# Block sums of the hidden state stored as high and low parts; value products in three passes

## The chip, the cores and the metric

One core of a Trainium2 chip runs the whole program in one launch. The metric is the time on the device in microseconds, the median of the runs. The core has five engines that matter here: TensorE (PE) multiplies matrices into PSUM; VectorE (DVE), ScalarE (ACT) and GpSimd (POOL) work elementwise, POOL without access to PSUM; SyncE (SP) issues the DMAs, in the order in which they stand in its queue. Each engine runs its own instructions in order and waits on semaphores for the others.

## The reference

A block of two layers works on 1024 tokens of width 1024, with 256 tokens of context ahead of them in the first layer. Everything is 32-bit floating point. What the change touches lies in the first layer:

```python
def mlstm_features(h, w_in, conv_w, conv_b, w_q, w_k, w_v):
    xm, z, og = jnp.split(h @ w_in, 3, axis=-1)
    xc = jax.nn.silu(short_conv(xm, conv_w, conv_b))
    q = headwise(xc, w_q)
    k = headwise(xc, w_k) * (MLSTM_HEAD_DIM ** -0.5)
    v = headwise(xm, w_v)
    return q, k, v, xc, z, og
...
    pre = (qkv @ w_g + b_g).astype(jnp.float32)
...
    y = jax.nn.sigmoid(og) * hn + skip * xc
    return (y * jax.nn.silu(z)) @ w_out
```

`h` is the normalised and modulated input, `headwise` a product with a block-diagonal matrix of 4 x 4 blocks. Four heads of width 512 then attend over the tokens, weighted with decays that come from the gates `pre`, forwards and backwards. The second layer (a pooling mixer) is not touched.

## The kernel before

**Products.** A matmul takes 32-bit operands that were rounded to a shorter type. To keep precision, each operand is held as a high part (the rounded value) and a low part (what the rounding left), and a product is three matmuls into one PSUM bank: high x high, high x low, low x high (`mm3`, L136). Each matmul has its own weight load, also where it repeats the one before. A weight tile is loaded from DRAM (tag `wr`), rounded on ACT (`wh`, L139), and DVE subtracts to get `wl` (L141).

**Stages.** The start-up (0 to 83 us) loads and normalises the input and modulates it on ACT and DVE (`modulate`, L306). The features follow (to some 355 us): 16 tiles `n` of 128 columns of `xm`, each a product over eight blocks of `h`, then a convolution. Behind tile `n`, `token_part(n)` makes the values and the gates' share of its tokens; it is a generator, and its pieces are put between the products of tile `n + 1` (one piece per six matmuls). A piece of 128 tokens is one matmul of 288 columns (high part against both parts of the weights) and one of 144; DVE adds the two halves out of PSUM (L400) into a tile of tag `T5`, and a store puts the 16 tiles into `v_d`. POOL adds `h` up from its parts in tiles 2 to 9 (L503) and SP stores it in `h_d`.

The plain stage (to some 411 us) makes the first two tiles of `z` and of `og` in the ordinary way. Between its products run the last token part, the steps of the gates (`gates`, at the counts `GATE_STEPS` of finished k-blocks: a chain of small DVE instructions, L442 to L453, then 20 transposes on PE, L460, which ACT copies out, L461, then scans on DVE) and `sums` at the counts `SUM_STEPS`: it loads `h_d` back into `T5` tiles (L516) and makes four block sums, each with high and low part (L520 to L527), in tiles `T_`.

The other 14 tiles of `z` and of `og` are made two at a time by `strassen` (to some 692 us): seven block products instead of eight, from two weight tiles `r1` (tag `wr`, L538) and `r2` (tag `T5`, L539) and sums of their blocks, which POOL makes (L543 to L546); each product's weights are rounded by ACT (L553) and DVE (L554).

Attention (692 to 1252 us) goes over four heads with eight query tiles each. In a head's first tile its `xc` is rounded (`cast_x`: ACT L651, and for heads 1 to 3 POOL's subtraction L652) and its values are loaded (`fetch_v`); in the second tile they are rounded in the same way (`cast_v`, five tiles of 1024 columns). In each tile, PE makes scores, DVE multiplies them by the decays (L731), normalises them (`weights`, L757 to L765), PE transposes them (L772), ACT and DVE split them (L774, L775), and PE multiplies by the values of the tile before (`values`).

**Order.** The order on PE is that of the code. On the other engines a scheduler sets it from the code when the program is built, and buffers are handed out by tag: 32 of `S4` (4 KB per partition), 5 of `T5`, 2 each of `wr`, `wh`, `wl`. A tile's first write waits for the last use of its buffer by the tile before.

## Time and profile before

| | us |
|---|---|
| median of 3 runs | 2089.25 |
| lowest and highest | 2087.11, 2090.32 |
| the profiled execution | 2086.98 |
| its span, first to last instruction | 2085.2 |

| engine | busy us | share of the span |
|---|---|---|
| PE | 1994.8 | 96% |
| PE weight loads | 1674.5 | 80% |
| DVE | 1329.5 | 64% |
| ACT | 772.6 | 37% |
| POOL | 475.4 | 23% |

The profile shows one execution. PE is busy nearly all the time, so the reading goes by stages: where PE is full, each added nanosecond of it counts, and where it is not, something else is waited for. Busy time of PE is not yet work done: its clock can be granted at half. DMA moves 272 MB, 131 GB/s in the mean.

### The profile page before, as it was taken

The numbers are of one execution on the slowest core, as the hardware profiler recorded it, in microseconds if no ns is written. First come the engines' busy times: TensorE is split into PE (matmuls) and PEld (weight loads), VectorE is DVE, ScalarE is ACT, GpSimd is POOL, SyncE is SP. The second block draws the span as 40 slices with busy tenths as digits, with TensorE's granted clock in tenths as the row PEclk, the third lists the DMA queues.
The fourth block names the chain that finished last, engine by engine and source line by source line (L and its number), as shares of the span: only waits on it lengthen the run. The fifth ranks groups of instructions, "written<-read, shape, count | busy, mean of one in ns | idle before, by whom it ended". The sixth has DMA issues, their size and how long they took to land.

```text
span 2085.2 us, 26407 instructions
## 1 busy us (share of the span) xinstructions
PE 1994.8 (96%) x10050; PEld 1674.5 (80%) x10050; DVE 1329.5 (64%) x2136; ACT 772.6 (37%) x1201; POOL 475.4 (23%) x482
## 2 busy tenths in 40 slices
PE   7899999799999899999999999999999999999998
PEld 5688888678888787778878888887888888888897
DVE  4877777877767868777677572354657273754444
ACT  5444444333334533333324232443423122224443
POOL 4411100032322313331333211252100000000275
PEclk9999999889999999999999999999999999999999
DMA  7233334444443636135234143434331212224473
GB/s 298 74 130 134 135 104 134 131 147 141 141 152 123 212 116 199 56 130 162 97 114 144 41 152 130 170 140 150 113 121 51 89 58 76 66 94 154 162 256 129
DMA packets 158335, 272.33 MB, mean 131 GB/s; under 512 B 10332, under 2 KB 89692, under 8 KB 158208
## 3 DMA queue, kind: packets, MB, share of 16 engines
q1 hardware_dynamic: 158208, 270.64, 39.1%
q8 instruction: 79, 1.29, 0.3%
q14 instruction: 48, 0.39, 0.1%
HBM read 205.41 MB, written 65.20 MB: 130 GB/s over the span
## 4 chain that ended last, share of the span: by engine, by line
PE 79%; DVE 12%; DMA 3%; issue 3%; POOL 2%; ACT 1%; SPq 0%; DVEq 0%; POOLq 0%; ACTq 0%
PE pa L133 40%; PE pc L133 31%; PE pb L133 6%; PE pb L772 1%; POOL S L961 1%; DMA wr<-in_w_ada_dram 1%; DVE S L306 1%; DVE wl L641 1%; DVE T L763 1%; DVE T L731 1%; POOL hn L941 1%; DVE T L765 1%; DVE S L304 1%; DVE den L759 1%; PE pc L803 1%
## 5 line engine op out<-in xcount | busy, mean ns | idle before, releaser
L133 PE MATMUL pa<-S,wh 128*128 128x512 f32 (+1 forms) x2496 | 723.5, 374 | 7.5 <-DVE S L306 7.2
L133 PEld LDWEIGHTS pa<-S,wh 128*128 128x128 f32 x2496 | 446.1, 190 | 81.3 <-DVE S L306 11.1
L133 PE MATMUL pc<-S,wh 128*128 128x512 f32 (+1 forms) x1616 | 454.9, 367 | 9.3 <-ACT wh L553 6.3
L133 PE MATMUL pa<-S,wl 128*128 128x512 f32 (+1 forms) x1248 | 460.6, 369 | 3.3 <-DVE wl L141 3.3
L133 PEld LDWEIGHTS pc<-S,wh 128*128 128x128 f32 x1616 | 294.6, 190 | 60.0 <-ACT wh L553 6.7
L141 DVE TENSOR_TENSOR wl<-wr,wh 128x1024 fp32r<-128x1024 f32 (+1 forms) x124 | 147.4, 1189 | 271.2 <-ACT wh L139 270.3
L133 PE MATMUL pc<-S,wl 128*128 128x512 f32 (+1 forms) x808 | 295.2, 367 | 3.9 <-DVE wl L554 2.9
L139 ACT ACTIVATE wh<-wr 128x1024 fp32r<-128x1024 f32 (+1 forms) x124 | 124.6, 1005 | 404.7 <-PE pa L133 183.4
L133 PEld LDWEIGHTS pa<-S,wl 128*128 128x128 f32 x1248 | 236.6, 190 | 44.2 <-DVE wl L141 3.7
L133 PE MATMUL pa<-S,S 128*128 128x512 f32 (+1 forms) x1152 | 251.1, 367 | 14.6 <-DVE T L731 14.6
L133 PE MATMUL pc<-S,pt 128*128 128x512 f32 x960 | 233.7, 397 | 0.0
L133 PEld LDWEIGHTS pa<-S,S 128*128 128x128 f32 x1152 | 195.7, 194 | 46.0 <-issue 11.6
L133 PEld LDWEIGHTS pc<-S,pt 128*128 128x128 f32 x960 | 179.5, 190 | 36.0
L133 PEld LDWEIGHTS pc<-S,wl 128*128 128x128 f32 x808 | 153.6, 190 | 29.9 <-DVE wl L554 3.6
L941 POOL TENSOR_TENSOR hn<-hn,pt 128x512 f32<-128x512 f32 (+1 forms) x48 | 77.5, 1615 | 300.7 <-ACT pt L940 290.3
L774 ACT ACTIVATE pt<-pb 128x512 fp32r<-128x512 f32 (+1 forms) x96 | 48.7, 522 | 176.1 <-PE pb L772 134.7
L400 DVE TENSOR_REDUCE T<-pb 128x144 f32<-128x288 f32 x160 | 72.1, 454 | 59.9 <-PE pb L133 59.6
L731 DVE SCALAR_TENSOR_TENSOR T<-pa,T 128x256 f32<-128x256 f32 (+3 forms) x184 | 76.5, 454 | 35.8 <-PE pa L133 30.4
L652 POOL TENSOR_TENSOR S<-S,S 128x1024 fp32r<-128x1024 f32 x35 | 89.3, 2569 | 41.6 <-ACT S L651 41.6
L553 ACT ACTIVATE wh<-T 128x512 fp32r<-128x512 f32 x70 | 42.4, 625 | 100.9 <-POOL T L546 56.7
L775 DVE TENSOR_TENSOR pt<-pb,pt 128x512 fp32r<-128x512 f32 (+1 forms) x96 | 56.5, 596 | 35.2 <-ACT pt L774 34.5
L133 PE MATMUL pb<-S,wh 128*128 128x512 f32 x256 | 78.8, 389 | 0.0
(322 smaller groups left out, 2511.5 us busy)
## 6 DMA issues: line engine op xcount, KB each, us to landing
wr<-in_bw_in_dram SPq DMA_DIRECT2D x40, 512.0 KB, 3.5
wr<-in_w_in_dram SPq DMA_DIRECT2D x34, 512.0 KB, 3.8
S<-xc_d SPq DMA_DIRECT2D x34, 512.0 KB, 5.2
wr<-in_w_ada_dram SPq DMA_DIRECT2D x32, 512.0 KB, 3.9
wr<-in_w_out_dram SPq DMA_DIRECT2D x32, 512.0 KB, 3.5
T<-in_bw_out_dram SPq DMA_DIRECT2D x32, 512.0 KB, 4.4
S<-y_d SPq DMA_DIRECT2D x28, 512.0 KB, 7.3
v_d<-T SPq DMA_DIRECT2D x16, 640.0 KB, 3.9
```

The costliest lines, as they stand in the source:

```text
L133: PE.matmul(out, lhsT, rhs, start=start, stop=stop)
L139: S.activation(h, r, AF.Copy)
L141: V.tensor_tensor(l, r, f(h), op=ALU.subtract)
L304: V.tensor_scalar(src, src, sc, sh, op0=ALU.mult, op1=ALU.add)
L306: V.tensor_tensor(lo, src[:, c], f(hi), op=ALU.subtract)
L400: V.tensor_reduce(vst[:, s], p.rearrange("p a b -> p b a"), axis=AX.X, op=ALU.add)
L553: S.activation(hi, a, AF.Copy)
L652: eng.tensor_tensor(t, f(t), f(u), op=ALU.subtract)
L731: V.scalar_tensor_tensor(W[:, lo + sh:hi + sh], p[:, lo - o:hi - o], 1.0, W[:, lo + sh:hi + sh], op0=ALU.mult, op1=ALU.mult, accum_out=dp[ ...
L774: S.activation(th[:, :n], p[:, :n], AF.Copy)
L775: V.tensor_tensor(tl_[:, :n], p[:, :n], f(th[:, :n]), op=ALU.subtract)
L941: G.tensor_tensor(acc, acc, sq, op=ALU.add)
```

## The change

The sums of `h` are no longer made in the plain stage. `modulate` stores `h` in `h_d` as soon as DVE has it. A generator `block_sums`, advanced twice in each feature tile from `n = 2` on, loads `h_d`, makes the sums and stores their high and low parts in a new tensor `t_d`; in the plain stage `load_sums` loads 16 tiles from there, one at every third count from 12 on, in the order in which the block products need them (`T_ORDER`). A value piece is three matmuls of 144 columns (`mm3`) into one bank that holds three pieces; ACT and DVE take high and low part out of it into two `T5` tiles, which are stored apart (`vh_d`, `vl_d`). `fetch_v` loads either; `cast_v` is gone. In `strassen` the product of `a12` comes second.

```diff
-        vst = tl("T5", [P, 10, 144])
-        for s in range(10):
...
-            p = pt_("pb", [P, 2, 144])
-            mm(p.rearrange("p a b -> p (a b)"), ah, vv.rearrange("p a b -> p (a b)"), True, False)
-            mm(p[:, 0], al, vv[:, 0], False, True)
-            V.tensor_reduce(vst[:, s], p.rearrange("p a b -> p b a"), axis=AX.X, op=ALU.add)
-        V.tensor_tensor(pre, pre, vst[:, :, P:], op=ALU.add)
-        nc.sync.dma_start(v_d[n // 4, :, :, (n % 4) * P:(n % 4 + 1) * P], vst[:, :, :P])
+        vh, vl = tl("T5", [P, 10, P], F32R), tl("T5", [P, 10, P], F32R)
+        for s0, s1 in ((0, 3), (3, 6), (6, 9), (9, 10)):
+            p = pt_("pb", [P, 3, 144])
+            for s in range(s0, s1):
...
+                mm3(p[:, s - s0], ah, al, vv[:, 0], vv[:, 1], True, True)
+            q = p[:, :s1 - s0]
+            S.activation(vh[:, s0:s1], q[:, :, :P], AF.Copy)
+            V.tensor_tensor(vl[:, s0:s1], q[:, :, :P], f(vh[:, s0:s1]), op=ALU.subtract)
+            V.tensor_tensor(pre[:, s0:s1], pre[:, s0:s1], q[:, :, P:], op=ALU.add)
+        for t, dst in ((vh, vh_d), (vl, vl_d)):
+            nc.sync.dma_start(dst[n // 4, :, :, (n % 4) * P:(n % 4 + 1) * P], f(t))
...
+    def block_sums():
+
+        for k in range(4):
+            t0, t1 = tl("S4", [P, T]), tl("S4", [P, T])
+            for t, kk in ((t0, k), (t1, k + 4)):
+                nc.sync.dma_start(t, h_d[kk])
...
+            for j, x in ((2, b11), (3, b22), (1, b12), (4, b21)):
+                t = tl("S4", [P, 2, 512], F32R)
+                S.activation(t[:, 0], x, AF.Copy)
+                V.tensor_tensor(t[:, 1], x, f(t[:, 0]), op=ALU.subtract)
+                nc.sync.dma_start(t_d[j - 1, k], f(t))
+                yield
...
-            if 2 <= n < 2 + KD:
-                hs = tl("S4", [P, T])
-                for hf in range(2):
-                    G.tensor_tensor(hs[:, hf * 512:hf * 512 + 512], f(h[n - 2, hf][0]), f(h[n - 2, hf][1]), op=ALU.add)
-                nc.sync.dma_start(h_d[n - 2], hs)
+            if n >= 2:
+                for _ in range(2):
+                    next(sums, None)
...
+        def load_sums(i):
+            j, k = T_ORDER[i // 4], i % 4
+            T_[j, k] = tl("S4", [P, 2, 512], F32R)
+            nc.sync.dma_start(f(T_[j, k]), t_d[j - 1, k])
...
-            u2 = plus(product("pc", s2, tpart(2)), p1)
-            u3 = plus(product("pa", s3, tpart(3)), u2)
-            done(0, 0, plus(product("pc", a12, b21), p1, p1))
+            done(0, 0, plus(product("pc", a12, b21), p1))
+            u2 = plus(product("pa", s2, tpart(2)), p1, p1)
+            u3 = plus(product("pc", s3, tpart(3)), u2)
...
-                        if count in SUM_STEPS:
-                            sums(SUM_STEPS.index(count))
+                        if count >= GATE_STEPS[0] and count % 3 == 0 and len(T_) < 16:
+                            load_sums(len(T_))
...
-    def cast_v(hd, eng):
-        hd["vh"] = [cast_low(t, [P, 2, DH], eng) for t in hd["vl"]]
...
-                fetch_v(hd, h)
+                fetch_v(hd, h, "vh")
...
-            cast_v(hd, G)
+            fetch_v(hd, h, "vl")
```

How the order of instructions moves is shown at three places. On DVE, in the plain stage, the gate chain before (names: `hn` holds the chain's values, `T` the tiles of `h` and `S` their sums, L520 to L527 are the sums, L580 is the end of a tile of `z`):

```order
L444 TENSOR_SCALAR hn_3324<-hn_3324 128x80
L520 TENSOR_TENSOR T_556_3347<-T_556_3347,T_555_3346 128x512
L445 RECIPROCAL hn_3324<-hn_3324 128x80
L521 TENSOR_TENSOR T_555_3346<-T_555_3346 128x512
L446 TENSOR_TENSOR hn_3324<-hn_3324 128x80
L522 TENSOR_TENSOR T_555_3346<-T_556_3347,T_555_3346 128x512
L447 TENSOR_TENSOR hn_3324<-hn_3324 128x80
L523 TENSOR_TENSOR T_556_3347<-T_556_3347,T_555_3346 128x512
L448 TENSOR_SCALAR hn_3324<-hn_3324 128x80
L580 TENSOR_TENSOR pt_3188<-pa_3374,pt_3188 128x512
L450 SCALAR_TENSOR_TENSOR hn_3324<-hn_3324 128x80
L527 TENSOR_TENSOR S_558_3351<-T_555_3346,S_558_3351 128x512
```

and after, where L451 to L458 are the chain's lines:

```order
L451 TENSOR_SCALAR hn_3512<-hn_3512 128x80
L452 RECIPROCAL hn_3512<-hn_3512 128x80
L453 TENSOR_TENSOR hn_3512<-hn_3512 128x80
L454 TENSOR_TENSOR hn_3512<-hn_3512 128x80
L455 TENSOR_SCALAR hn_3512<-hn_3512 128x80
L457 SCALAR_TENSOR_TENSOR hn_3512<-hn_3512 128x80 x5
L593 TENSOR_TENSOR pt_3367<-pa_3544,pt_3367 128x512
L457 SCALAR_TENSOR_TENSOR hn_3512<-hn_3512 128x80
L458 SCALAR_TENSOR_TENSOR hn_3512<-hn_3512 128x80
L460 SCALAR_TENSOR_TENSOR T_487_3505<-hn_3512,xf 128x20x4
```

The instructions of the sums have left the chain; one end of a `z` tile still stands in it.

On SP, before, from the plain stage's middle to the first load of `r2` (L539, the last row; L516 loads `h` for the sums, L538 is `r1`, L590 and L593 load and store for `og`):

```order
L516 DMA T_581_3493<-h_d 128x1024
L516 DMA T_582_3494<-h_d 128x1024
L538 DMA wr_3849<-in_w_in_dram 128x1024
L479 DMA a_d<-T_554_3342 36x1280
L590 DMA hn_3569<-xc_d 128x512
L516 DMA T_591_3546<-h_d 128x1024
L593 DMA ga_d<-hn_3566 128x4x128
L593 DMA gb_d<-hn_3569 128x4x128
L590 DMA hn_3602<-xc_d 128x512
L516 DMA T_592_3547<-h_d 128x1024
L539 DMA T_617_3703<-in_w_in_dram 128x1024
```

and after, where L540 loads the stored sums (the last two of 16), L551 is `r1` and L552 is `r2`:

```order
L540 DMA S_535_3787<-t_d 128x1024
L540 DMA S_539_3807<-t_d 128x1024
L551 DMA wr_3840<-in_w_in_dram 128x1024
L552 DMA T_545_3841<-in_w_in_dram 128x1024
L551 DMA wr_3987<-in_w_in_dram 128x1024
L603 DMA hn_3695<-xc_d 128x512
L486 DMA a_d<-T_491_3530 36x1280
L606 DMA ga_d<-hn_3692 128x4x128
L552 DMA T_570_3988<-in_w_in_dram 128x1024
```

The first `r2` stood behind all loads of `h` and two stores of `og` results; it now stands ahead of the first load and store for `og`, behind the loads of the sums.

On POOL, in the second query tile of head 1, before (L652 is the subtraction of the casts, L790 and L806 belong to the query tile, L742 to L751 to the decays):

```order
L790 TENSOR_TENSOR rs__1264_7295<-mv_7292,mhalf 128x1
L652 TENSOR_TENSOR S_1239_7159<-S_1239_7159,S_1283_7384 128x1024
L806 TENSOR_TENSOR hn_7404<-hn_7404,ab_7256 128x512
L652 TENSOR_TENSOR S_1240_7161<-S_1240_7161,S_1284_7387 128x1024
L742 MEMSET dp_7629 128x8
L652 TENSOR_TENSOR S_1241_7163<-S_1241_7163,S_1285_7390 128x1024
L652 TENSOR_TENSOR S_1242_7165<-S_1242_7165,S_1286_7393 128x1024
L652 TENSOR_TENSOR S_1243_7167<-S_1243_7167,S_1287_7396 128x1024
L751 AFFINE_SELECT T_1362_7806<-T_1362_7806 128x128
```

and after, from the same instruction of the query tile on (L800, before L790):

```order
L800 TENSOR_TENSOR rs__1192_7428<-mv_7425,mhalf 128x1
L816 TENSOR_TENSOR hn_7532<-hn_7532,ab_7389 128x512
L761 AFFINE_SELECT T_1290_7934<-T_1290_7934 128x128
L752 MEMSET dp_7757 128x8
L760 AFFINE_SELECT T_920_5999<-T_920_5999 128x128
L800 TENSOR_TENSOR rs__1225_7600<-mv_7597,mhalf 128x1
L752 MEMSET dp_7935 128x8
```

The five subtractions are gone; the rows of the query tile and of the decays follow each other directly.

## Rows read from the trace of the kernel before

**Rows 1.** Busy time of each engine in a stretch of the features:

```profile
core 0: us, PE busy (x) PEld busy (x) DVE busy (x) ACT busy (x) POOL busy (x), PEclk, DMA share, GB/s
200.00:250.00 50.00, 50.00 (x284) 42.73 (x283) 34.75 (x66) 21.78 (x31) 5.55 (x13) 1.00 0.37 123
```

**Rows 2.** PE in order of time: start us, us, form; around one value piece:

```profile
199.75 0.62 PE L133 MATMUL pa<-S,wh 128*128 128x512 f32 x2
200.21 0.39 PE L133 MATMUL pa<-S,wl 128*128 128x512 f32 x1
200.44 0.36 PE L133 MATMUL pb<-vv,S 128*128 128x288 f32 x2
200.64 0.67 PE L133 MATMUL pa<-S,wh 128*128 128x512 f32 x2
201.16 0.39 PE L133 MATMUL pa<-S,wl 128*128 128x512 f32 x1
```

**Rows 3.** PE's weight loads in order of time, same place:

```profile
200.58 0.30 PEld L133 LDWEIGHTS pa<-S,wh 128*128 128x128 f32 x2
200.92 0.19 PEld L133 LDWEIGHTS pa<-S,wl 128*128 128x128 f32 x1
```

**Rows 4.** Busy time in two stretches of the plain stage and its end:

```profile
370.00:385.00 15.00, 9.57 (x37) 6.26 (x36) 13.53 (x26) 6.46 (x13) 0.00 (x0) 0.66 0.21 71
410.00:430.00 20.00, 10.82 (x32) 7.82 (x31) 15.69 (x18) 7.86 (x13) 10.17 (x7) 0.66 0.58 168
```

**Rows 5.** PE's waits, 340 to 460 us: total us, times, longest:

```profile
PE pc L133 <- ACT wh L553: 6.3, 1, 6.3
PE pb L460 <- DVE T L453: 3.7, 1, 3.7
PE pc L133 <- DVE wl L554: 2.9, 1, 2.9
PE pb L460 <- ACT T L461: 1.7, 2, 1.4
```

**Rows 6.** DVE in order of time: two subtractions of the sums:

```profile
371.56 1.29 DVE L527 TENSOR_TENSOR S<-T,S 128x512 fp32r<-128x512 f32 x2
```

**Rows 7.** SP's queue in order of time: the first `r2`:

```profile
405.51 0.38 SPq L539 DMA_DIRECT2D T<-in_w_in_dram  x1
```

**Rows 8.** Busy time behind the start of heads 1 and 3:

```profile
850.00:875.00 25.00, 21.31 (x105) 18.04 (x104) 19.08 (x41) 10.77 (x19) 14.65 (x11) 0.93 0.12 32
...
1138.00:1163.00 25.00, 21.31 (x94) 17.64 (x93) 17.58 (x38) 9.72 (x18) 13.74 (x12) 0.86 0.11 32
```

**Rows 9.** PE's waits, 690 to 1260 us (attention):

```profile
PE pa L133 <- DVE T L731: 14.6, 4, 3.7
...
PE pb L772 <- DVE pt L775: 6.9, 4, 2.5
```

**Rows 10.** POOL in order of time: three subtractions of head 1's casts:

```profile
857.28 7.78 POOL L652 TENSOR_TENSOR S<-S,S 128x1024 fp32r<-128x1024 f32 x3
```

**Rows 11.** DVE in order of time: the same two lines beside those casts, and after:

```profile
855.18 2.76 DVE L763 TENSOR_SCALAR T<-T,den 128x1152 f32<-128x1152 f32 x1
...
860.26 2.56 DVE L765 SCALAR_TENSOR_TENSOR T<-T,den,T 128x256 f32<-128x256 f32 x1
...
866.00 0.75 DVE L763 TENSOR_SCALAR T<-T,den 128x1024 f32<-128x1024 f32 x1
...
867.06 0.48 DVE L765 SCALAR_TENSOR_TENSOR T<-T,den,T 128x256 f32<-128x256 f32 x1
```

**Rows 12.** PE in order of time: value products of head 0, then of head 1:

```profile
835.76 6.06 PE L133 MATMUL pc<-S,pt 128*128 128x512 f32 x26
855.39 0.39 PE L133 MATMUL pc<-S,pt 128*128 128x512 f32 x1
```

**Rows 13.** DMA issues: count, KB each, median us to landing; values stored and loaded:

```profile
v_d<-T SPq DMA_DIRECT2D x16, 640.0 KB, 3.9
S<-v_d SPq DMA_DIRECT2D x20, 512.0 KB, 8.7
```

More of the change, by code (lines that the diff above doesn't have):

```diff
@@ L38 @@
 GATE_STEPS = (12, 15, 27, 50)
-SUM_STEPS = (16, 24, 32, 40)
+T_ORDER = (2, 3, 1, 4)
 ORDER_B = ("u0", "u1", "b0", "u2", "b1", "u3", "z0", "b2", "z1", "b3", "p0", "z2", "p1", "z3", "p2", "p3")
@@ L122, in hybrid_block @@
     xc_d = dr.tile([KE, P, TA], F32, name="xc_d")
-    v_d = dr.tile([NH, P, 10, DH], F32, name="v_d")
+    vh_d = dr.tile([NH, P, 10, DH], F32, name="vh_d")
+    vl_d = dr.tile([NH, P, 10, DH], F32, name="vl_d")
     h_d = dr.tile([KD, P, T], F32, name="h_d")
+    t_d = dr.tile([4, 4, P, 2, 512], F32, name="t_d")
     y1_d = dr.tile([KE, P, T], F32, name="y1_d")
@@ L298, in hybrid_block, with modulate @@
         G.tensor_tensor(dst[:, :, 16:32], gsum[:, i], f(dst[:, :, 0:16]), op=ALU.subtract)
-    def modulate(src, parts, k, j):
+    def modulate(src, parts, k, j, dst=None):
         sc, sh = gs0[:, k, j:j + 1], mod0[:, k, 0, j:j + 1]
@@ L304, in modulate @@
         V.tensor_scalar(src, src, sc, sh, op0=ALU.mult, op1=ALU.add)
+        if dst is not None:
+            nc.sync.dma_start(dst, src)
         for hi, lo, c in parts:
@@ L315, in hybrid_block @@
                 h[k, hf] = tuple(t[:, k % 2] for t in quad[hf])
-            modulate(x_sb[k], [(*h[k, hf], slice(512 * hf, 512 * hf + 512)) for hf in range(2)], k, 0)
+            modulate(x_sb[k], [(*h[k, hf], slice(512 * hf, 512 * hf + 512)) for hf in range(2)], k, 0, h_d[k])
         else:
@@ L320, in hybrid_block @@
                 h[k, hf] = tuple(t[:, 512 * hf:512 * hf + 512] for t in pair)
-            modulate(x_sb[k], [(*pair, slice(0, T))], k, 0)
+            modulate(x_sb[k], [(*pair, slice(0, T))], k, 0, h_d[k])
     hch = [tl("S4", [P, 4, TC], F32R) for _ in range(2)]
@@ L490, in gates @@
         S.activation(emt, p, AF.Exp, scale=-1.0)
-    side, parts = iter(()), []
+    def block_sums():
[3 more added lines that the diff above has]
+                nc.sync.dma_start(t, h_d[kk])
+            b11, b12, b21, b22 = t0[:, :512], t0[:, 512:], t1[:, :512], t1[:, 512:]
+            V.tensor_tensor(b22, b22, b12, op=ALU.subtract)
+            V.tensor_tensor(b12, b12, b11, op=ALU.subtract)
+            V.tensor_tensor(b11, b22, b11, op=ALU.add)
+            V.tensor_tensor(b21, b21, b11, op=ALU.subtract)
+            yield
+            for j, x in ((2, b11), (3, b22), (1, b12), (4, b21)):
[3 more added lines that the diff above has]
+                nc.sync.dma_start(t_d[j - 1, k], f(t))
+                yield
+    side, parts, sums = iter(()), [], block_sums()
     with ctx0:
@@ L511, in hybrid_block @@
         T_ = {}
-        def sums(k):
-            t0, t1 = tl("T5", [P, T]), tl("T5", [P, T])
-            for t, kk in ((t0, k), (t1, k + 4)):
-                nc.sync.dma_start(t, h_d[kk])
-            b11, b12, b21, b22 = t0[:, :512], t0[:, 512:], t1[:, :512], t1[:, 512:]
-            for j in range(1, 5):
-                T_[j, k] = tl("S4", [P, 2, 512], F32R)
-            V.tensor_tensor(b22, b22, b12, op=ALU.subtract)
-            V.tensor_tensor(b12, b12, b11, op=ALU.subtract)
-            V.tensor_tensor(b11, b22, b11, op=ALU.add)
-            V.tensor_tensor(b21, b21, b11, op=ALU.subtract)
-            for j, x in ((2, b11), (3, b22), (1, b12), (4, b21)):
-                t = T_[j, k]
-                S.activation(t[:, 0], x, AF.Copy)
-                V.tensor_tensor(t[:, 1], x, f(t[:, 0]), op=ALU.subtract)
+        def load_sums(i):
+            j, k = T_ORDER[i // 4], i % 4
+            T_[j, k] = tl("S4", [P, 2, 512], F32R)
+            nc.sync.dma_start(f(T_[j, k]), t_d[j - 1, k])
         def tpart(j):
```

17 lines of the change are left out of this document (8 added, 9 removed).

## The prediction

> **What bounds the kernel now.** I read the stages first: a table of busy time in stretches tells where TensorE (PE) is short of its time. While the features are made it is not: in 200 to 250 us PE is busy 50.00 of 50 us at granted clock 1.00, with VectorE (DVE) at 34.75 and ScalarE (ACT) at 21.78 [rows 1]. Each nanosecond that the change adds to PE there is paid, and work on DVE and ACT is free as long as nothing waits for it. The second read is of the two stretches in which PE is not full. Busy time times clock is what PE did; the rest is lost. The clock has two levels, 1.2 and 2.4 GHz (0.50 and 1.00); 0.66 is a mixture, and before it fell PE had idled, for 3.7 us at the first place and 6.3 at the second [rows 5]. At 370 to 385 us: 15 - 9.57 x 0.66 = 8.7 us lost; at 410 to 430: 20 - 10.82 x 0.66 = 12.9 us [rows 4]. The waits behind that are four lines: 3.7 us for the gate chain on DVE (L453), 1.7 for ACT's copies of the transposes (L461), 6.3 and 2.9 for the cast weights of the first block product (L553, L554) [rows 5]. The third read is of the heads. Behind the start of head 1 PE loses 25 - 21.31 x 0.93 = 5.2 us, behind head 2 the same (its row reads alike), behind head 3 25 - 21.31 x 0.86 = 6.7 us, 17.1 us together [rows 8]; what PE waits for is DVE's product with the decay matrix (L731) [rows 9]. The last 830 us, which the change does not touch, are left out.
>
> **Value products: a cost on PE.** Before, a block of 128 tokens takes a matmul of 288 columns and one of 144; after, three of 144. The columns are the same 432, the weight loads are three in place of two, and there are 16 x 10 = 160 blocks. What a block costs PE now is read from starts [rows 2]. The matmul behind the pair starts at 200.64, 0.20 us after the pair at 200.44. That is not all: the two matmuls of 512 columns behind it take from 200.64 to 201.16, 0.52 us, where two others take 0.46 (199.75 to 200.21). The pair costs 0.20 + 0.06 = 0.26 us. The weight loads show why: two loads behind the pair take 0.30 us together, one alone 0.19, so the second began 0.11 us after the first [rows 3]. They load the same matrix twice, so a repeated load is not spared. A matmul of 144 columns passes in less than that. I therefore price each of the three at one spacing of loads: 3 x 0.11 = 0.33 us, 0.07 to 0.08 more than now; with 0.08, 160 x 0.08 = 13 us. All 160 stand between full-width matmuls of a stage in which PE has no idle time, so nothing hides it. Bounds: 0, if equal columns mean equal time, and 160 x (0.36 - 0.25) = 18 us with both readings at the ends of their rounding. I take 13, since rows 3 measure just this.
>
> The Trainium skill speaks against the change too (TensorE: Matmul & The Clock Gate, LDWEIGHTS): a load takes its column count over 1.2 ns, an estimated 107 ns for 128 columns. The trace agrees with 0.11. The same page (Back-to-back issue gap) gives about 81 ns per matmul for 128 columns in a sustained stream; by that figure three would cost an estimated 0.24 us and the change about nothing. No row here shows 81.
>
> **What the value products free and add elsewhere.** Per feature tile, DVE loses ten reductions and gains four subtractions and four small adds from PSUM, ACT gains four copies, and a second store of 640 KB goes out; with 15 and 28 us spare per 50 [rows 1] I count 0. PSUM buffers turn over four times per tile and not ten, and hold three blocks each; PE fills the next while one is emptied.
>
> **Block sums and h.** Before, GpSimd (POOL) adds h up again in the features and it is stored from there; after, it is stored in the start-up, where DVE makes it anyway. Eight DMAs enter SP's queue among loads of the weights of n = 2 and later, needed a tile or more afterwards: 0, and from -1 to +3 as bounds. The sums (32 subtractions and adds, 16 casts) move from the plain stage to the features of n = 2 on. They are hidden there by the same spare time. If that cover were gone, the case is the third rival.
>
> **The two waits around the plain stage.** The DVE order has eight instructions of the sums inside the gate chain (the first five are in the rows shown of it); two of them take 1.29 us [rows 6], so eight take some 5.2 us, more than PE's wait of 3.7. Without them the chain ends before PE asks. The second wait begins with a load: the second weight tile of the first block product is issued at 405.51 [rows 7], since its buffer was in the hands of the sums. In the changed order it stands right behind the loads of the stored sums and waits for the gate transposes, which PE has behind it by 385 us [rows 4]. It goes out some 20 us earlier, and GpSimd's sums of weight blocks and the casts follow it. Besides, the product that needs only the first tile now comes second. Of 8.7 + 12.9 = 21.6 us I keep 1.7 (ACT's copies stay) and about 1 for the clock around them: **-19 us**. Bounds: 12.9, if only the waits on L453, L553 and L554 go and the clock stays; 21.6, if all goes. What is late next: the 16 loads of 512 KB of stored sums go ahead of the first product's weights in SP's queue. They wait for buffers of the last feature tiles, whose matmuls lie ahead of the gate transposes, so before 370 us [rows 4]; some 40 us remain for 8 MB.
>
> The other 15 block products get the new order too. Their weights are cast a product ahead, and in the list of waits L553 and L554 stand once each, for the first block product alone [rows 5]: 0.
>
> **The casts at the heads.** At 857.28 three subtractions of GpSimd run one behind the other for 7.78 us [rows 10]. In that time DVE's scaling takes 2.76 us and its two-input update 2.56 us; at 866 and 867 us, with GpSimd done, 0.75 and 0.48 [rows 11]. So DVE's chain is some 4 us late there from two instructions alone, which is the PE wait: 14.6 us in four, the longest 3.7 [rows 9]. One of the four is head 0's; for it I count nothing. The change replaces these casts by five more loads per head, and the GpSimd order shows the five gone. The other 15 subtractions (of xc) stay, and with them the waits elsewhere in the heads. Gain: the 17.1 us of heads 1 to 3, and for head 0 half of its 2.5 us wait on L775, the longest of that line [rows 9], because a weight load and its use crowd that stretch: **-18.3 us**. Bounds: 3 x 3.7 = 11, if the clock gives nothing back, and 19.6.
>
> Who waits for the new loads: the value products of the next tile. Their buffers come free with the 26 products that run from 835.76 to 841.8, and the first use is at 855.39 [rows 12]. Loads of this kind land after 8.7 us in the median [rows 13]: 850.5, 4.9 us early. I count 0; twice as slow would be 3.8 us late in every head.
>
> **The sum.** From the profiled execution, 2087.0 us (span 2085.2): -19 - 18.3 + 13 = -24.3, so 2062.7. The median of the three runs is 2.3 us above that execution; in its terms **2065 us**.
>
> **Rivals.** (a) Loads late: the low parts land 17.4 us after their buffers are free, PE waits 3.8 us in each of four heads, and most of the 18.3 is given back: 2080. For it: ten loads per head in place of five, and the DMA share of 0.11 to 0.12 [rows 8] is without them. Against: 4.9 us in hand [rows 12, 13]. (b) Products for nothing: columns set the price, not loads. For it: the 0.20 us from start to start. Against: the 0.52 behind it. 2065 - 13 = 2052. By the 81 ns of the Trainium skill's page it would be nearly this. (c) Slower: the stores in the features. A tile now takes four of the five T5 buffers (two value tiles in place of one), and DVE's low part may be written only after the store of the tile before has landed; those stores stand in SP's queue among the new stores of sums, each of which waits for DVE. If each of the ten tiles n = 2 to 11 waits for one landing of 3.9 us [rows 13], that is 39 us on PE: 2104. It decides from (2089 - 2065) / 10 = 2.4 us per tile on. Against: the store before is some 18 us old by then. (d) The change does not do what it says at the plain stage: 8 MB of loads or GpSimd's chain hold the first product as the sums did; the 12.9 us stay: 2078.
>
> **How the numbers follow.** Forecast 0.60, (a) 0.14, (b) 0.10, (c) 0.09, (d) 0.07. The forecast's own range is 2065 with +5 for the products at 18, +6 for the plain stage at 12.9, +7 for the heads at 11, and -13, -3, -1 the other way. Taking in (a), (b) and (d) and leaving out (c): 2048 to 2083. About 0.2%, 4 us, is what can be told from no change: faster 0.88, same 0.04, slower 0.08, the last from (c).
>
> **What the changed profile would show.** Products: windows at 200 to 250 still at 50.00, with the plain stage beginning some 13 us later, and PEld rows behind three 144s at 0.11 spacing. Sums: no PE wait on the gate chain or on the first product's casts, clock 1.00 at the entry of the block products. Heads: no L731 wait behind heads 1 to 3, and DVE's scaling at 0.75 to 0.9 us throughout. Wrong would be the forecast if PE waits for a DMA in the value products (a), if the features take no longer (b), or if PE in the features falls below 50 of 50 (c).

## The result

The changed kernel takes **2065.22 us** in the median of four runs (2063.48 to 2065.69); the kernel before took 2088.63 beside it (2087.11 to 2090.32). The ratio is 0.9886, with a 95% interval of 0.9869 to 0.9903. The forecast was 2065, range 2048 to 2083: faster, as forecast. The profiled execution took 2063.48 us, 23.5 less than that of before.

**Where the time went.** The stages have borders on PE that both traces show. Each row of the next fence is one line of the code on PE: operation, tiles, count, duration in ns (min/median/max), first and last start in us. The first two are before and after at the end of the features, the next two the first transposes of attention, the last two its end:

```profile
L426 PE MATMUL pb<-ident,T x10: 221/222/247, 361.6 to 362.2; 32*128 32x32 f32 x10
...
L433 PE MATMUL pb<-ident,T x10: 220/221/243, 380.3 to 380.8; 32*128 32x32 f32 x10
...
L772 PE MATMUL pb<-ident,T x320: 270/272/421, 712.4 to 1257.3; 128*128 128x128 f32 x160
...
L782 PE MATMUL pb<-ident,T x320: 270/272/423, 712.5 to 1232.9; 128*128 128x128 f32 x160
...
L803 PE MATMUL pa<-ident,hn x4: 272/272/273, 1271.1 to 1271.4; 128*128 128x128 f32 x4
...
L813 PE MATMUL pa<-ident,hn x4: 271/272/273, 1246.2 to 1246.5; 128*128 128x128 f32 x4
```

The first value product starts at 98.4 us before and at 99.5 after. So the features take 263.2 and 280.7 us, **+17.5**; the way from there to attention (gates, plain stage, block products) 350.8 and 332.2, **-18.6**; attention 559.0 and 534.0, **-25.0**. With +1.1 ahead of the features and +1.5 from attention's end to that of the program, where nothing was changed, the sum is -23.5. Forecast were +13, -19 and -18.3.

The stretches after, as [rows 1, 4, 8] show them before (the plain stage now begins some 18 us later, so 370 to 385 is still features and is left out, and the entry of the block products lies in 400 to 430):

```profile
core 0: us, PE busy (x) PEld busy (x) DVE busy (x) ACT busy (x) POOL busy (x), PEclk, DMA share, GB/s
200.00:250.00 50.00, 50.00 (x285) 42.64 (x284) 33.99 (x60) 26.79 (x44) 0.47 (x9) 1.00 0.63 213
...
400.00:430.00 30.00, 28.76 (x139) 23.64 (x138) 22.68 (x25) 9.85 (x15) 13.75 (x8) 1.00 0.64 203
850.00:875.00 25.00, 25.00 (x125) 20.81 (x124) 10.06 (x36) 5.09 (x11) 2.81 (x6) 1.00 0.25 80
1138.00:1163.00 25.00, 25.00 (x135) 21.30 (x134) 14.70 (x40) 8.91 (x18) 4.85 (x9) 1.00 0.23 64
```

PE is at 50.00 in the features as before, at clock 1.00 at the entry of the block products (0.66 before), and full behind the starts of heads 1 and 3 (21.31 at 0.93 and 0.86 before). Its waits from 95 to 690 us, all of them, which answer to [rows 5]: line, what it waited for, total us, times, longest:

```profile
PE pa L135 <- DVE pt L368: 2.7, 1, 2.7
PE pb L492 <- DVE T L487: 1.2, 1, 1.2
PE pb L467 <- ACT T L468: 0.7, 3, 0.3
PE pb L467 <- DVE T L460: 0.2, 1, 0.2
```

The waits on the gate chain (now L460: 0.2 us, 3.7 before) and on the first block product's weights (9.2 before) are gone; a new one, on L368, stands at the top. In attention, 690 to 1260 us, as [rows 9]:

```profile
PE pb L782 <- ACT T L772: 7.4, 3, 3.0
PE pa L135 <- DVE T L741: 6.4, 3, 4.8
PE pb L782 <- DVE pt L785: 4.4, 3, 1.9
PE pb L782 <- DVE mod L160: 1.7, 2, 1.1
PE pc L813 <- DVE hn L802: 0.5, 1, 0.5
```

That is 20.4 us; before there were 34.7 (14.6 on the product with the decays, 7.4, 6.9, 4.7, 0.9 and 0.2). One wait on the decays lies ahead of the border, at 702 us (3.5 before, 4.8 after); behind it 31.2 and 15.6 us are left, so 15.6 of the 25.0 are waits. Most of the rest is the half clock that followed them: busy time times what the granted clock lacked of 1.00, summed over windows of 2.5 us, falls from 11.1 to 2.9 us. Of the four waits on the decays the three of 3.7 us are gone; two small ones, 1.6 together, are new, where the casts of `xc` run.

**A value piece, after.** PE in order of time, then its loads (start us, us, form), which answer to [rows 2] and [rows 3]:

```profile
202.09 0.45 PE L135 MATMUL pb<-vv,S 128*128 128x144 f32 x3
202.38 0.67 PE L135 MATMUL pa<-S,wh 128*128 128x512 f32 x2
202.89 0.40 PE L135 MATMUL pa<-S,wl 128*128 128x512 f32 x1
```

```profile
201.87 0.53 PEld L135 LDWEIGHTS pb<-vv,S 128*128 128x128 f32 x3
202.31 0.30 PEld L135 LDWEIGHTS pa<-S,wh 128*128 128x128 f32 x2
```

The matmul behind the piece starts 0.29 us after it, and the two behind take 0.51 (202.38 to 202.89) where others take 0.46: 0.34 us a piece, against 0.26 before and 0.33 forecast. The two loads behind the piece take 0.30 us together, one alone 0.19: they are 0.11 us apart, as before.

**What held the features besides.** DVE in order of time (in brackets how long it stood idle before, and for what), and the load that it waited for in SP's queue:

```profile
136.76 0.69 DVE L506 TENSOR_TENSOR S<-S,S 128x512 f32<-128x512 f32 x1 [2.08 <-DMA S<-h_d]
...
141.92 0.42 DVE L368 TENSOR_TENSOR pt<-pa,pt 128x256 fp32r<-128x256 f32 x1
...
142.85 1.29 DVE L368 TENSOR_TENSOR S<-pa,S 128x512 fp32r<-128x512 f32 x2
```

```profile
131.37 0.95 SPq L504 DMA_DIRECT2D S<-h_d  x2
```

The first of the moved sums follows its loads directly in the code, and DVE stood 2.08 us for them. Behind it in DVE's queue stood the three instructions of L368, which end a feature product and which PE needed. Which of the two PE paid for, the load or the place of L368 behind the sums, is asked below, under "A step between the load of `h` and the sums".

### The profile page after: what moved, and what is told of

It is laid out like the page before. It is cut to its first block, busy times and chain, and to the rows that moved or that the text cites. A ratio compares the mean times of both kernels' runs of the same rounds, so it can differ in the third digit from the quotient of the medians.

```text
span 2061.8 us, 26868 instructions
## 1 busy us (share of the span) xinstructions
PE 1992.7 (97%) x10210; PEld 1678.4 (81%) x10210; DVE 1264.2 (61%) x2088; ACT 778.9 (38%) x1245; POOL 406.4 (20%) x446
## 4 chain that ended last, share of the span: by engine, by line
PE 83%; DVE 6%; DMA 3%; POOL 2%; issue 2%; ACT 1%; SPq 0%; DVEq 0%; POOLq 0%; ACTq 0%
PE pa L135 43%; PE pc L135 31%; PE pb L135 6%; PE pb L782 1%; DMA wr<-in_w_ada_dram 1%; POOL S L971 1%; POOL hn L951 1%; DVE wl L654 1%; PE pc L813 1%; DMA S<-a_d 0%; DVE S L883 0%; DMA T<-in_bw_out_dram 0%; DVE wl L143 0%; POOL S L970 0%; DVE den L769 0%
## 5 line engine op out<-in xcount | busy, mean ns | idle before, releaser
L135 PE MATMUL pc<-S,pt 128*128 128x512 f32 x960 | 228.8, 393 | 0.0
L795 DVE BATCH_NORM_STATS2 st<-pc 128x6 f32<-128x512 f32 x32 | 22.3, 697 | 99.6 <-PE pc L135 99.6
L143 DVE TENSOR_TENSOR wl<-T,wh 128x1024 fp32r<-128x1024 f32 x32 | 45.5, 1422 | 46.7 <-ACT wh L141 46.6
L816 POOL TENSOR_TENSOR hn<-hn,ab 128x512 f32<-128x512 f32 x32 | 46.1, 1440 | 132.8 <-DVE hn L815 85.3
```

Source lines behind the costliest of these rows:

```text
L135: PE.matmul(out, lhsT, rhs, start=start, stop=stop)
L143: V.tensor_tensor(l, r, f(h), op=ALU.subtract)
L795: V.bn_stats(b6, pv)
L816: G.tensor_tensor(ht, ht, ab[1], op=ALU.add)
```

## Experiments

Every version ran beside the kernel before on the same chip, and is judged by its ratio to that. Stage times are worked out from the starts of PE's rows, by the borders above; in the table attention is counted to the end of its last row, 0.3 us more.

| version | median us | ratio and interval | features | to attention | attention |
|---|---|---|---|---|---|
| before | 2088.63 | 1 | 263.2 | 350.8 | 559.2 |
| after | 2065.22 | 0.9886 [0.9869, 0.9903] | 280.7 | 332.2 | 534.3 |
| e1_two_pass | 2059.77 | 0.9874 [0.9858, 0.9890] | 278.5 | 329.4 | 538.7 |
| e2_narrow | 2063.38 | 0.9890 [0.9874, 0.9907] | 280.3 | 328.9 | 534.5 |
| e3_casts_only | 2071.74 | 0.9926 [0.9912, 0.9941] | 265.6 | 352.0 | 535.4 |
| e4_sums_only | 2075.96 | 0.9949 [0.9935, 0.9964] | 268.4 | 333.0 | 559.2 |
| e5_pool_reads | 2070.65 | 0.9895 [0.9879, 0.9911] | 280.7 | 335.2 | 536.7 |
| e6_pool_writes | 2066.92 | 0.9879 [0.9865, 0.9894] | 281.1 | 333.1 | 535.3 |
| e7_old_order | 2071.87 | 0.9902 [0.9886, 0.9919] | 280.7 | 333.9 | 537.8 |
| e8_load_ahead | 2061.93 | 0.9855 [0.9840, 0.9870] | 275.9 | 331.1 | 537.8 |
| e9_two_pass_ahead | 2052.66 | 0.9826 [0.9805, 0.9848] | 267.8 | 333.7 | 538.4 |
| e10_pool_reads_more | 2077.18 | 0.9948 [0.9931, 0.9966] | 280.8 | 332.6 | 547.2 |
| e11_castx_dve | 2047.04 | 0.9806 [0.9788, 0.9824] | 275.9 | 331.4 | 524.1 |
| e12_cast_writes | 2096.84 | 1.0049 [1.0030, 1.0069] | 263.2 | 348.1 | 568.9 |

Between versions in which nothing of a stage was edited, attention varies by some 4 us (534.3 to 538.7), the way to attention by 6 (328.9 to 335.2), the second layer by 4 (804.5 to 808.6) and the features by 0.4 (280.7 to 281.1); smaller differences are not read. Much of the scatter in attention is in the clock: after and e8_load_ahead have the same order on PE there and nearly the same idle time of it (15.6 and 14.7 us), but the clock took 2.9 us from one and 7.5 from the other. So the -25.0 of after lies at the good end of what the scatter allows.

### The parts one by one

**The casts alone**, put into the kernel before. The value products stay two matmuls and a reduction; the result is split:

```diff
-        nc.sync.dma_start(v_d[n // 4, :, :, (n % 4) * P:(n % 4 + 1) * P], vst[:, :, :P])
+        vh, vl = tl("T5", [P, 10, P], F32R), tl("T5", [P, 10, P], F32R)
+        S.activation(vh, vst[:, :, :P], AF.Copy)
+        V.tensor_tensor(vl, vst[:, :, :P], f(vh), op=ALU.subtract)
+        for t, dst in ((vh, vh_d), (vl, vl_d)):
+            nc.sync.dma_start(dst[n // 4, :, :, (n % 4) * P:(n % 4 + 1) * P], f(t))
...
-            cast_v(hd, G)
+            fetch_v(hd, h, "vl")
```

> The kernel before with only the casts of the values moved: the values are split in the feature stage out of the reduced tile and stored as high and low part, the heads load both and cast nothing. Value products in two passes and block sums in the plain stage as before. If the gain in the heads belongs to the casts alone, the time from the first transpose of head 0 to the last of head 3 falls from 559 to 534 us, and the kernel is 18 to 25 us below before, 2064 to 2071. Rival: the low parts would come late without the rest of the change, or the splits cost time in the features: less than 15 us gained.

Attention falls by 23.8 us, the way to it does not change (+1.2), the features cost 2.4. So attention's whole gain belongs to the casts, and it is larger than the 18.3 of the sum. By the ratio the kernel gains some 15 us, less than the 18 to 25 expected.

**The sums alone**, also in the kernel before: `h_d` stored by `modulate`, `block_sums` and `load_sums` as in the change, values and order of products as before.

```diff
-                if count in SUM_STEPS:
-                    sums(SUM_STEPS.index(count))
+                if count >= GATE_STEPS[0] and count % 3 == 0 and len(T_) < 16:
+                    load_sums(len(T_))
```

> The kernel before with only the block sums moved: h stored at the start-up, sums made in the features and stored, loaded in the plain stage; value products, casts and the order of the block products as before. If the plain stage's gain belongs to the sums: 18 to 19 us below before, less what the first sums hold up in the features (3.6 us in the changed kernel), so some 15 us, 2074. If the order of the first block product is needed for it: PE still waits at the entry of the block products and at most 8 us are gained, 2081.

The way to attention falls by 17.8 us, attention stays at 559.2, and the features cost 5.2. So the 18.6 belong to the sums. By the ratio the kernel gains some 11 us where 15 were expected, as the features cost more than the 3.6 allowed for. Their price stands in its waits, 95 to 690 us:

```profile
PE pa L134 <- DVE pt L367: 2.3, 1, 2.3
PE pa L134 <- DVE S L367: 1.2, 1, 1.2
```

In the total the two parts add up: gains of 0.0074 and 0.0051 together make a ratio of 0.9875, and e1_two_pass (below), which joins them, has 0.9874. By stages they do not: the features cost 2.4 and 5.2 us apart and 15.3 together (278.5 against 263.2), and other stages happened to make up for it.

### The price of three passes

**Fewer columns.** One of the three passes is cut to 16 columns; its loads stay. The low x high term of the values is left out but for these.

```diff
-                mm3(p[:, s - s0], ah, al, vv[:, 0], vv[:, 1], True, True)
+                mm(p[:, s - s0], ah, vv[:, 0], True, False)
+                mm(p[:, s - s0, :16], al, vv[:, 0, :16], False, False)
+                mm(p[:, s - s0], ah, vv[:, 1], False, True)
```

> The changed kernel with the low x high pass of the value products cut from 144 columns to 16 (the low parts then go only into the gate columns; the values lose their low x high term). The number of matmuls and weight loads is unchanged. Theory 1, weight loads 0.11 us apart set the price: no difference from the changed kernel, 2065 within 2, and the features take as long. Theory 2, columns set the price: 128 columns less in 160 blocks, 0.053 us each at 2.4 GHz, 8.5 us below it, about 2057.

The features take 280.3 us in place of 280.7. 128 of a pass's 144 columns are worth nothing here: the load sets the price, and rival (b) falls.

**Fewer loads.** The change with the two matmuls of 288 and 144 columns and the reduction of before, the result split at the end as in e3_casts_only.

> The changed kernel with the value products of before: one matmul of 288 columns and one of 144 per block, the halves added by DVE out of PSUM (160 reductions), the sum then split into high and low part by ACT and DVE and stored as in the changed kernel. Theory 1, weight loads set the price of the third pass (0.08 us in each of 160 blocks): some 13 us below the changed kernel, about 2052, if DVE, which gets 72 us of reductions back, keeps up. Theory 2, the 432 columns set the price: as the changed kernel, 2065. Theory 3, DVE becomes the bound of the features with the sums and the reductions together: above 2065, and PE falls below 50 of 50 us there.

The expected 13 us did not come: the features take 278.5, only 2.2 less. PE is no longer full in the features:

```profile
200.00:250.00 50.00, 45.83 (x236) 38.50 (x235) 39.01 (x67) 24.11 (x34) 0.31 (x6) 0.93 0.60 211
```

and it waits twice for L368, 2.8 us at 142 and 4.2 us at 236 us. DVE, with ten reductions a tile again and the sums on top, is busy 39.01 of 50 us (34.75 before). Ahead of the first wait DVE stood 0.55 us for the load of `h`; ahead of the second, the longer one, it did not stand for a load at all, but the sums again ran ahead of L368.

**A step between the load of `h` and the sums.** One line in `block_sums`, so that the loads stand one advance of the generator ahead of the sums:

```diff
             for t, kk in ((t0, k), (t1, k + 4)):
                 nc.sync.dma_start(t, h_d[kk])
+            yield
```

in the change (e8_load_ahead) and in the two-pass version (e9_two_pass_ahead):

> The changed kernel with the loads of h for a set of block sums issued one step before the first subtraction (24 steps in place of 20, two per feature tile). In the changed kernel PE stands 2.7 us at 142 us behind DVE, which stood 2.1 us for the first load of h. If that load is the cause: the wait and the half clock behind it go, 3 to 4 us below the changed kernel, 2061 to 2062, and the features take 277 us in place of 280.7. If DVE is too full at this place whatever the load does: the wait stays, 2065.

> The two-pass value products of e1 together with the early loads of e8. If the stalls that ate e1's gain came from the loads of h alone: the features take 277 - 13 = 264 us and the time is some 2049. If DVE, at 41 to 42 of 50 us in e1, is too full for reductions and sums together: PE still waits for it in the features, 270 to 276 us there, and the time is 2055 to 2062, little or nothing below e8.

The first has features of 275.9 us, 4.8 less than after, and the wait on L368 is gone. But the edit did not bring the load forward. Both advances stand in the same feature tile, so loads and sums still follow each other. SP and DVE in e8_load_ahead:

```profile
129.96 0.96 SPq L504 DMA_DIRECT2D S<-h_d  x2
```

```profile
134.07 0.69 DVE L368 TENSOR_TENSOR S<-pa,S 128x512 fp32r<-128x512 f32 x1 [0.67 <-ACT S L367]
135.34 0.69 DVE L507 TENSOR_TENSOR S<-S,S 128x512 f32<-128x512 f32 x1 [0.58 <-DMA S<-h_d]
```

This execution runs 1.41 us ahead of after's (first value product at 98.12 against 99.53). With that added the loads go out at 131.37 and the first sum starts at 136.75, to 0.01 us as in after. What changed is DVE's order: two of the three instructions of L368 (130.81 and 134.07) now stand ahead of the sum, one of them in the time in which DVE had stood for the load. e4_sums_only says the same from the other side: its first sum starts at 134.26 without a wait for the load, the sums run ahead of L367, and PE still waits 2.3 us. So what PE paid for is the place of the sums ahead of the product's end in DVE's queue. The expectation's test, load or full DVE, was not made: the load came when it did before, and DVE was as full as before (33.24 of 50 us from 200 us on, against 33.99).

What is left over before, 12.7 us, is the price of the products: 160 x 0.079 us; PE has no idle time in these features, and 0.2 us in those of before. So the +17.5 are 12.7 for the products and 4.8 for a stall that the forecast had at 0: 2.7 of waiting, 1.7 of clock behind it (0.74 and 0.58 granted in the two 2.5 us from 142.5 on), and 0.4 that the trace does not place.

The second has 267.8 us: the two-pass form does save 8.1 us over the three-pass one, not 12.7. DVE is busy 42.26 of 50 us there, and PE stands idle for 3.2 us, 1.6 of them at the stage's end; the rest of the difference stays open. Its ratio is 0.9826, against 0.9855 of e8_load_ahead.

### The order of the block products

The change with the old order of the first three products (`s2`, `s3`, `a12`).

> The changed kernel with the order of the seven block products as before (the sum s2 second, s3 third, a12 fourth). If the order matters only for the first block product's entry: PE waits there for GpSimd's sums, at most 3 us, and the other 15 are unchanged: 2065 to 2068. If it matters in all 16: more than 5 us above 2065.

333.9 in place of 332.2 us, within the scatter; and e4_sums_only, which keeps the old order, has 333.0. The order is not needed for the gain, and what it is worth by itself cannot be told.

### What the casts cost

The prediction's account was contention: DVE's scaling is slow beside GpSimd's subtractions, so PE's wait. Three versions put work on GpSimd into the changed kernel, behind the second load of values: five subtractions per head of the casts' size (e5_pool_reads), twelve memsets (e6_pool_writes), twelve subtractions (e10_pool_reads_more). None of the results is used.

```diff
             fetch_v(hd, h, "vl")
+            scr = tl("S4", [P, T])
+            for c in (0, 1, 2, 3, 0):
+                G.tensor_tensor(scr, f(hd["xl"][c]), f(hd["xh"][c]), op=ALU.subtract)
```

> The changed kernel with five subtractions of 128 x 1024 on GpSimd added in the second query tile of each head, of the size and at the place of the casts that the change removed, from two tiles of the head into a scratch tile that nobody reads. No engine waits for their results. Theory 1, the casts cost because GpSimd's reads hold DVE up: DVE's scaling takes 2 us and more there again, PE's waits on the product with the decay matrix come back behind heads 1 to 3, and the time goes up by 15 to 25 us, to 2080 or more. Theory 2, PE waited for the cast values themselves: no waits come back, 2065 within 3.

DVE's scaling (now L773) is slow again beside the subtraction. The two-input updates that follow it are not, but no subtraction runs beside them: GpSimd stands for a small instruction of the decays, and its next three begin at 857.08:

```profile
853.15 2.78 DVE L773 TENSOR_SCALAR T<-T,den 128x1152 f32<-128x1152 f32 x1
...
856.23 0.48 DVE L775 SCALAR_TENSOR_TENSOR T<-T,den,T 128x256 f32<-128x256 f32 x1
```

```profile
852.92 2.39 POOL L857 TENSOR_TENSOR S<-S,S 128x1024 f32<-128x1024 f32 x1
...
857.08 7.33 POOL L857 TENSOR_TENSOR S<-S,S 128x1024 f32<-128x1024 f32 x3
```

And PE does not mind: busy all the time, attention 2.4 us longer, within the scatter. The miss is plain; the slow scaling alone makes no wait in the new order. PE's rows in the changed kernel show why (behind 852 us, head 1):

```profile
852.24 1.52 PE L135 MATMUL pc<-S,pt 128*128 128x512 f32 x6
853.60 0.39 PE L135 MATMUL pa<-S,S 128*128 128x512 f32 x1
853.82 1.52 PE L135 MATMUL pc<-S,pt 128*128 128x512 f32 x6
855.19 0.27 PE L782 MATMUL pb<-ident,T 128*128 128x128 f32 x1
855.21 3.00 PE L135 MATMUL pc<-S,pt 128*128 128x512 f32 x12
```

24 value products stand in a row, with two other matmuls between, 6 us of work that needs nothing of DVE's chain. In the kernel before only seven stand ahead of the wait (one at 855.39, [rows 12], and the six of the first row here), and the next six behind it:

```profile
857.68 1.55 PE L133 MATMUL pc<-S,pt 128*128 128x512 f32 x6
859.07 1.11 PE L133 MATMUL pa<-S,S 128*128 128x256 f32 x8
863.87 0.93 PE L133 MATMUL pa<-S,S 128*128 128x512 f32 x3 [3.69 <-DVE T L731]
```

With the casts gone the scheduler puts the value products earlier, and DVE's chain has room.

> The changed kernel with twelve fills of a scratch tile of 128 x 1024 added on GpSimd at the same place: GpSimd is occupied but reads nothing. Theory 1a, it is the reading of two tiles beside DVE that holds DVE up: DVE's scaling stays at 0.75 to 0.9 us, at most GpSimd's own small instructions come later, and the time stays within 5 us of 2065. Theory 1b, it is enough that GpSimd is occupied (its small instructions of the decays come late, and PE waits through them): 2075 and more, as with reads.

Memsets cost still less: attention 535.3 us. The scaling takes 1.30 us beside one memset; nine more run when DVE has nothing of this chain to do.

> The changed kernel with twelve of the added subtractions of e5 in place of five, so that GpSimd reads without a gap through the stretch in which DVE normalises the first scores of a head. In e5 one of DVE's three instructions was held up there, and no wait came back. Theory 1 with alignment, each instruction of DVE waits for the running subtraction and PE has some 4 us of slack: three or more are held up now, DVE is 6 us late, and waits of 3 us and more come back behind heads 1 to 3, 12 to 20 us in all: 2077 to 2085. Theory 2, GpSimd's reads were not what PE waited for: no waits, 2065 to 2070 as e5.

Twelve subtractions cost 12.9 us of attention, 10.3 of them in head 0, where one wait of PE on DVE (L802) takes 6.9 us. Behind the starts of heads 1 to 3 there is again no wait. So the time lies in the range of the first theory, but not for its reason. At head 0 DVE has weights to make besides, and four subtractions run there in one stretch of 12.54 us. The order on PE moved in this version too (some 2270 of the 2765 matmuls of attention stand as in after; in e5_pool_reads and e6_pool_writes over 2730), so the 12.9 us cannot be put to GpSimd's reads alone.

**The other way round:** the kernel before with its PE order nearly kept, and `cast_v`'s subtraction replaced by three memsets of GpSimd. The low parts are zero.

```diff
-        hd["vh"] = [cast_low(t, [P, 2, DH], eng) for t in hd["vl"]]
+        hd["vh"] = []
+        for t in hd["vl"]:
+            u = tl("S4", [P, 2, DH], F32R)
+            S.activation(u, f(t), AF.Copy)
+            eng.memset(f(t), 0.0)
+            eng.memset(f(t), 0.0)
+            eng.memset(f(t), 0.0)
+            hd["vh"].append(u)
```

> The kernel before, where GpSimd's subtraction of each value cast is replaced by three fills of the same tile with zeros (the low parts of the values are left out, the products with them run as before). The order on TensorE stays nearly that of before, GpSimd is occupied somewhat longer (three fills of 0.96 us for a subtraction of 2.4) and the low tiles are ready no earlier, but GpSimd reads nothing. Theory 1, reads beside DVE make the waits: DVE's scaling falls from 2.76 to 1.3 us or less at the start of heads 1 to 3, the waits on the product with the decay matrix (3.7 us each) go, and the heads take some 15 to 20 us less, 540 to 545 in place of 559: 2069 to 2074. Theory 2, the place of the value products in TensorE's order or the late low tiles make them: the waits stay, 2085 to 2092.

The waits did not go, they grew. This kernel's lines are those of before plus 7 (L738 is the product with the decays, L770 to L772 the scaling and its updates):

```profile
PE pa L133 <- DVE T L738: 17.1, 4, 4.5
PE pb L779 <- DVE pt L782: 8.6, 6, 2.5
```

DVE behind the start of head 1:

```profile
853.76 7.34 DVE L770 TENSOR_SCALAR T<-T,den 128x1152 f32<-128x1152 f32 x1
...
861.35 0.34 DVE L771 SCALAR_TENSOR_TENSOR T<-T,den,T 128x128 f32<-128x128 f32 x1
861.60 0.47 DVE L772 SCALAR_TENSOR_TENSOR T<-T,den,T 128x256 f32<-128x256 f32 x1
```

GpSimd beside it, rows of a stretch without a gap:

```profile
853.25 0.96 POOL L680 MEMSET S<- 128x1024 f32 x1
...
859.52 0.96 POOL L681 MEMSET S<- 128x1024 f32 x1
860.43 0.81 POOL L758 TENSOR_SCALAR_AFFINE_SELECT T<-T 128x128 f32<-128x128 f32 x1
861.19 0.94 POOL L681 MEMSET S<- 128x1024 f32 x1
```

and PE:

```profile
855.49 3.18 PE L133 MATMUL pa<-S,S 128*128 128x512 f32 x19
863.12 4.12 PE L133 MATMUL pa<-S,S 128*128 128x512 f32 x10 [4.45 <-DVE T L738]
```

The scaling ended at 861.10 us, only after the chain of memsets that had begun before it (the last of them ends at 860.48; the next starts at 861.19): 7.34 us for what takes 0.75 alone [rows 11]. It is held by instructions of GpSimd that only write, too, while the updates with two inputs run freely beside them (0.34 and 0.47 us; beside subtractions they took 2.15 and 2.56, the second of them in [rows 11]). So "beside subtractions" was too narrow, and the expectation failed for that reason: the cause was not removed. Scaling and updates took 8.15 us together, 7.47 before.

Nor is the longer wait the scaling's. DVE's chain ended earlier than before here (PE goes on at 863.12, before at 863.87). But PE had run out of other work at 858.7 us, before at 860.2, since six value products had now moved behind the wait: 4.45 us in place of 3.69 is PE's order.

The Trainium skill (SBUF — State Buffer, SBUF: two separate sides) says that GpSimd and DVE share a port pair that one instruction holds to its end, and that DVE asks for it in a two-port mode, against any GpSimd instruction, or with two SBUF inputs, against one that reads. The rows agree as to who is held by what: L771 and L772 pass the memsets, L770 does not; that L770 runs in a two-port mode no row shows. How often a held instruction can be passed over the section does not tell; L770 waited through eight memsets, not one.

**The other casts.** If contention and PE's order both count, the casts of `xc`, which stay on GpSimd, should cost something where PE is still short. e8_load_ahead with `cast_x`'s subtraction on DVE in every head:

```diff
-    cast_x(hd, G if h else V)
+    cast_x(hd, V)
```

> The kernel of e8 with the other 15 subtractions (those of xc at the start of heads 1 to 3) moved from GpSimd to DVE, as head 0 has them: five of 1.2 us in place of five of 2.4, and nothing reads beside DVE. If the waits that stay at the start of heads 1 to 3 (DVE's scaling 2.4 us there in the changed kernel) belong to these reads as well: some 3 us less per head, 9 in all, 2052. If DVE is the bound there, 6 us more work on it: the waits grow, 2062 to 2070.

Attention falls to 524.1 us, 13.7 below e8_load_ahead and 10.2 below after. A stretch beside those casts, in e8_load_ahead and then in e11_castx_dve (columns as above):

```profile
780.00:815.00 35.00, 31.45 (x157) 25.78 (x156) 29.34 (x71) 6.97 (x12) 7.46 (x8) 0.95 0.57 179
```

```profile
780.00:815.00 35.00, 34.63 (x187) 29.48 (x186) 30.52 (x79) 9.88 (x18) 4.38 (x7) 1.00 0.62 191
```

In the second row PE is busy for 3.2 us more, and the clock stays at 1.00 in place of 0.95. DVE's scaling and updates of 2.35 to 2.61 us beside those casts are gone, and PE's waits in attention fall from 14.7 to 5.7 us. Nearly all of PE's order is as in e8_load_ahead (some 2630 of 2765 matmuls). The casts' results also come sooner, 1.2 us each in place of 2.4, and the run does not part that from the contention. At 2047.04 us this is the fastest version run, faster than both kernels. Whether the two-pass form adds to it was not run.

## Why the prediction was right

**Products, +13: measured 12.7.** The step held as written: one more load at 0.08 us in a stage without idle PE, the columns up to 144 free. e2_narrow shows the second half, e8_load_ahead the sum. Of the 81 ns for 128 columns, the Trainium skill's figure under which three matmuls would have cost about nothing (TensorE: Matmul & The Clock Gate, Back-to-back issue gap), no run shows anything: a piece of three took 0.34 us, 0.11 each, and three in place of two cost 0.079 us.

**Moved work in the features, 0: measured 4.8.** This is the step that failed. "They are hidden there by the same spare time" was argued from DVE's busy share; but each engine runs its instructions in order, and the sums were put ahead of L368, which PE needed, whatever DVE's share. The first sum also stood 2.08 us for its load, but the load is not what PE paid for: with the load and the sum at the same moments and two of the three L368 ahead of them, PE does not wait (e8_load_ahead), and without a wait for the load it does (e4_sums_only, and the second wait of e1_two_pass). It is near rival (c): DVE is late in the features, not for the stores, which hurt nobody, but for the place of the sums in its queue. The row shown is the one stall that the trace names, 2.7 us on PE; that another order gives back 4.8 is the run's. The exchange of ten reductions for four subtractions and four small adds was counted at 0 as well; e1_two_pass and e9_two_pass_ahead show that it had a worth: with the reductions and the sums together, DVE holds PE up.

**Gates and first block product, -19: measured -18.6 in the change, -17.8 with the sums alone.** Chain, casts and clock went as written: PE's idle time falls by 11.3 us and what the clock takes by 8.2 (windows of 2.5 us). ACT's copies kept 0.7 us in place of 1.7. The stage scatters by 6 us, so that the agreement to 0.4 is in part luck, and what the new order of the products is worth, which the sum did not price apart, stays open. Rival (d) falls.

**Heads, -18.3: measured -25.0.** The term was mis-sized and half its mechanism was missing. From the first transpose of a head to that of the next, the last to the border, the gains are 4.3, 7.0, 5.5 and 8.1 us: 20.6 in heads 1 to 3, where 17.1 were counted, and 4.3 in head 0, where 1.2 was. PE is full behind the starts of heads 1 to 3. What came on top (of which the scatter of the clock may hold some 4) is in the waits on L775 and on `mod`, which fell from 11.6 to 6.1 us, and in the clock. The account of DVE's delay counted two instructions; L764 between them took 2.15 us as well (0.35 alone), so the three were 5.9 us late and not 4. The missing half is in PE's order. The part on the kernel ahead of the prediction says that PE's order is that of the code. **That is wrong** for everything from the plain stage to the end of attention: in the code PE is ordered by hand only up to the features' end and in the second layer, and between them the scheduler orders PE as well. Taking the casts away therefore moved the value products on PE itself. The runs show that slow scaling alone makes no wait once PE has those products to do (e5_pool_reads, e6_pool_writes), and that in nearly the old order a held scaling goes with waits as long as before or longer (e12_cast_writes). For the casts of `xc`, in a nearly unchanged order, taking them from GpSimd gave 10 us or more (e11_castx_dve). What stays open is the fourth case, the old order without contention, and with it how the 25 us divide between the two. Rival (a) falls: no wait of PE on the low parts' loads stands in the lists. One sign did not come: the scaling was to take 0.75 to 0.9 us throughout, but beside the casts of `xc`, which stay on GpSimd, it still takes up to 2.45 us.

So the time was hit closer than its terms, by luck: 4.8 us forgotten in the features and 6.7 us too little gain in attention nearly cancel.

## What to carry to other kernels

Price a small matmul in a full stage by its weight loads, not by its columns: 16 columns cost here what 144 did. Spare time in the mean does not hide work that stands in an engine's queue ahead of something PE needs: see what stands behind it. Another place in the queue was worth 4.8 us here. Before blaming a slow elementwise instruction for PE's wait, see what else PE could do in that time, and who orders it; then try to take GpSimd's long instructions, writes too, away from DVE's chain: moving one more cast to DVE gave 10 us or more.

## What the hardware showed

One thing was not expected: a scaling on DVE with one tile as input took 7.34 us beside a chain of memsets on GpSimd (0.75 alone), and the two-input updates right behind it were not held at all. Another was forecast, and is worth keeping: a matmul of 16 columns in place of 144 saved nothing that could be told in 160 places (280.3 against 280.7 us); its weight load stayed.
